# Column tiles of the array for the HGRN scores, and new buffer offsets in SBUF

## The chip, the cores and the metric

One core of a Trainium2 chip. A core has a matrix engine (TensorE, PE in the profile; its weight loads are shown apart as PEld), VectorE (DVE), ScalarE (ACT), GpSimd (POOL) and SyncE (SP), which issues most of the DMAs. They share SBUF, 128 partitions of on-chip memory; TensorE writes to PSUM, 128 partitions of eight banks. The metric is the time of one execution on the device in microseconds, as the median of several runs.

## What is computed

A trunk of two decoder layers on 256 positions of width 2048, float32. Layer 0 mixes positions with an HGRN2 recurrence of 16 heads (key and value width 128), layer 1 with a causal gMLP. After each mixer comes a gated ConvFFN of width 5632; every sub-layer ends in a layer norm of the scaled residual plus the sub-layer. The part that the change touches is the recurrence:

```python
cum = jnp.cumsum(lf_c, axis=2)
rel = cum[:, :, :, None, :] - cum[:, :, None, :, :]
decay = jnp.exp(jnp.where(mask[:, :, None], rel, -jnp.inf))
scores = jnp.einsum('bhtk,bhsk,bhtsk->bhts', q_c, k_c, decay)
out = (jnp.einsum('bhts,bhsv->bhtv', scores, v_c)
       + jnp.einsum('bhtk,bhkv->bhtv', q_c * jnp.exp(cum), state))
```

So the score of query t and key s is a product over the key width in which each channel has decayed from s to t; scores with s after t are zero. The kernel has its own scheme for this: it takes 128 positions at a time and builds the scores in levels.

## The kernel before

**The large matmuls.** Weights come from HBM in chunks of 512 rows by 512 columns (1 MB), one DMA on SyncE's queue each. `convert` (L80) splits a chunk `raw` into a high part `whi` (a cast on ScalarE, L90) and the remainder `wlo` (a subtraction on VectorE, L91); the pool `wp` has three buffers each of `raw`, `hi` and `lo`, and `ahead` (L96) keeps up to three chunks converted ahead of use. The activations stand split in the same way: `X` (input of a sub-layer, transposed) and `Y` (input of its last projection), each as 16 blocks of 128 rows with 256 high and 256 low columns.

`block_a` (L107) has the activations as stationary operand and streams 512 columns of weights: three matmuls in a row, high by high, high by low, low by high (L120 to L122), called a trio here. `block_b` (L147) has the weights as stationary operand and streams the activations: `both` (L156) 512 columns under a high weight, `rest` (L163) 256 columns under a low one; the two are called a pair. A block_b of four chunks has 64 pairs, a block_a of four chunks 32 trios. In the whole program 240 chunks go through block_b (16 pairs each) and 152 through block_a or its staggered form (8 trios each).

**Where the buffers start.** The pool `cp` holds, in the order of the code, a pad of `LINE - 128` bytes, X, Y (32 KB each per partition), z (16 KB), a pad of `PAD1` bytes, then small constants. The pool `wp` follows. A `whi` or `wlo` buffer has `SKEW` elements (of four bytes) more than it needs, so that the three buffers of a tag start 8320 bytes apart.

**The HGRN stage.** `hgrn` (L440) runs four groups of four heads. A group (L457) is a block_b for q, one for f, a block_a for v, two calls of `mix` (L521; two heads and 256 positions each, called halves), a block_b for the gate sg, and the output's norm. The tile framework orders the instructions of all engines ahead of time from dependencies and priorities, so the small matmuls of `mix` stand in TensorE's queue between pairs of the sg block; each engine then takes its queue in order.

**mix.** It works on four 128-position squares th (two heads by two position blocks), with decayed queries Q, keys K and segment decays T. All its matmuls are float32, which the profile records as two instructions each.

- The diagonal, `pd` (L533 to L544): sixteen matmuls of 32 stationary columns by 32 moving ones, each at its own column tile of the array, `tile_position=(0, 32 * j)`, and four predicated copies through the identity into `scores`.
- Three levels, b = 1, 4, 16 (L545 to L587): at each, blocks of 4b positions are joined from four parts. W (L550 to L554) holds the moving columns, 192 for each square; four matmuls (L558) of 128 keys by 192 columns follow, in two PSUM tiles `pl` of two squares each, and six predicated copies (L567) with `mask` put the wanted strips into `scores`. Then Q, K and T are carried to the next level (L571 to L587).
- The last product (L589 to L594): four matmuls of 128 by 128 for the 64 by 64 corner, and a predicated copy with `upper`.
- The product between the two position blocks (`pc`, L604), the product with v (`pout`, L611 to L616), its copy to `o` (L617), and four squares with a running sum on ScalarE into the scratch tile `junk` (L622).

`scores`, set to zero once, has two buffers, one for each half. PSUM's pool `misc` has two banks for all of these; `acc` has six for the large matmuls. `masks` (L415) makes the masks on GpSimd at the start; `bounds` (L278) uses the tile `lbt` in the buffer of tag "sg".

Of the kernel before, what the change touches and what calls it, by code (L numbers as in the profile page):

```python
# [8 lines left out]
F32 = mybir.dt.float32  # L9
F32R = mybir.dt.float32r  # L10
U32 = mybir.dt.uint32
AF = mybir.ActivationFunctionType
ALU = mybir.AluOpType
PSUM = bass.MemoryType.PSUM

P = 128
# [12 lines left out]
LEVELS = (1, 4, 16)  # L29
FFN_GROUPS = (3, 4, 4)  # L30
AHEAD = 3
LINE = 512
PAD1 = 192
SKEW = 32
XSEQ = ((0, 2, 4), (2, 2, 0), (4, 4, 1), (8, 4, 1), (12, 4, 0))
TURN_ACT = 3

# [1 line left out]
class Trunk:  # L39
# [4 lines left out]
    def __init__(self, ctx, tc, a):  # L44
        self.tc = tc
        self.nc = nc = tc.nc
        self.a = a
        self.ctx = ctx
        ent = ctx.enter_context
        self.cp = ent(tc.tile_pool(name="cp", bufs=1))  # L50
        self.wp = ent(tc.tile_pool(name="wp", bufs=3))
        self.acc = ent(tc.tile_pool(name="acc", bufs=6, space=PSUM))
        self.misc = ent(tc.tile_pool(name="misc", bufs=2, space=PSUM))
        cp = self.cp
        cp.tile([P, LINE - 128], mybir.dt.uint8, name="pad0")
        self.X = cp.tile([P, NK, 2, S], F32R, name="X")
        self.Y = cp.tile([P, NK, 2, S], F32R, name="Y")
        self.z = cp.tile([P, 2, D], F32, name="z")
        cp.tile([P, PAD1], mybir.dt.uint8, name="pad1")
        self.small = ent(tc.tile_pool(name="small", bufs=2))  # L60
        self.plan = []
        self.issued = 0
        self.taken = 0
        self.ready = []
# [15 lines left out]
    def convert(self, raw, extra, pieces=2):  # L80
        nc = self.nc
        pool = self.xp if extra else self.wp
        size = CK * NB + (0 if extra else SKEW)
        hi = pool.tile([P, size], F32R, tag="hi", name="whi")
        lo = pool.tile([P, size], F32R, tag="lo", name="wlo")
        hi, lo = (x[:, : CK * NB].rearrange("p (k n) -> p k n", k=CK) for x in (hi, lo))
        n = CK // pieces
        for i in range(0, CK, n):
            s = slice(i, i + n)
            nc.scalar.copy(hi[:, s, :], raw[:, s, :])  # L90
            self.last_lo = nc.vector.tensor_tensor(  # L91
                lo[:, s, :], raw[:, s, :], hi[:, s, :].bitcast(F32), ALU.subtract
            )
        self.ready.append((hi, lo))
# [317 lines left out]
        for c in range(4):  # L412
            self.want(wo, 3 * CK, c * NB, c == 3)

    def masks(self):  # L415


        nc, cp = self.nc, self.cp
        self.mask = {}
        for b in LEVELS:  # L420
            n = P // 4 // b
            m = cp.tile([P, n, 3, b], F32, name=f"mask{b}")
            nc.gpsimd.memset(m, 1.0)
            nc.gpsimd.affine_select(
                out=m, in_=m, pattern=[[-4 * b, n], [-b, 3], [0, b]], compare_op=ALU.is_ge,
                fill=0.0, base=0, channel_multiplier=1,
            )
            nc.gpsimd.affine_select(
                out=m, in_=m, pattern=[[4 * b, n], [b, 3], [0, b]], compare_op=ALU.is_ge,
                fill=0.0, base=b - 1, channel_multiplier=-1,  # L430
            )
            self.mask[b] = m
        self.upper = cp.tile([P, 1], F32, name="upper")
        nc.gpsimd.memset(self.upper, 1.0)
        nc.gpsimd.affine_select(
            out=self.upper, in_=self.upper, pattern=[[0, 1]], compare_op=ALU.is_ge,
            fill=0.0, base=P // 2 - 1, channel_multiplier=-1,
        )

    def hgrn(self):  # L440
        nc, tc = self.nc, self.tc
        w = self.a["hg_w_in"][0]
        with ExitStack() as st:
            hp = st.enter_context(tc.tile_pool(name="hp", bufs=1))
            lp = st.enter_context(tc.tile_pool(name="lp", bufs=2))
            h1 = st.enter_context(tc.tile_pool(name="h1", bufs=1))
            self.load_vectors(h1.tile([P, 8, P], F32, tag="o", name="rows"))
            self.masks()
            scores = []
            for i in range(2):  # L450
                s = h1.tile([P, 3, 2, P], F32, name=f"scores{i}")
                nc.gpsimd.memset(s, 0.0)
                scores.append(s)
            for g in range(4):
                self.hgrn_group(g, w, hp, lp, h1, scores)

# [64 lines left out]
    def mix(self, q, f, k1, v, sc, o, ss, lp, h1):  # L521
# [3 lines left out]

        nc = self.nc
        flat = lambda x: x.rearrange("p h n -> p (h n)")
        own = lambda th: slice((th % 2 * 2 + th // 2) * P, (th % 2 * 2 + th // 2 + 1) * P)
        K, T = flat(k1), flat(f)
        Q = lp.tile([P, 2 * S], F32, tag="Q", name="Q")  # L530
        nc.vector.tensor_tensor(Q, flat(q), T, ALU.mult)
        scv = sc[:, 0:2].rearrange("p t h n -> p (t h) n")
        pd = self.misc.tile([P, 4, 32], F32, tag="m", name="pd")  # L533
        for th in range(4):
            for j in range(4):
                own_j = slice(own(th).start + 32 * j, own(th).start + 32 * j + 32)
                nc.tensor.matmul(
                    pd[32 * j : 32 * j + 32, th, :], K[:, own_j], flat(q)[:, own_j],
                    start=True, stop=True, tile_position=(0, 32 * j),
                )  # L540
        for j in range(4):
            s = slice(32 * j, 32 * j + 32)
            mi = self.ident[s, s].bitcast(U32).unsqueeze(1).to_broadcast([32, 4, 32])
            nc.vector.copy_predicated(scv[s, :, s], mi, pd[s])  # L544
        for b in LEVELS:  # L545
            n = 2 * S // (4 * b)
            seg = lambda x: x.rearrange("p (n i r) -> p n i r", i=4, r=b)
# [2 lines left out]
            W = lp.tile([P, 4, 192], F32, tag="W", name="W", bufs=1)  # L550
# [1 line left out]
            nc.scalar.copy(Wv[:, :, 0:3, :], Qv[:, :, 1:4, :])  # L552
            nc.vector.tensor_tensor(Wv[:, :, 3:5, :], Qv[:, :, 2:4, :], row(Tv[:, :, 1:3]), ALU.mult)
            nc.vector.tensor_tensor(Wv[:, :, 5:6, :], Wv[:, :, 4:5, :], row(Tv[:, :, 1:2]), ALU.mult)  # L554
            for t in range(2):
                pl = self.misc.tile([P, 2, 192], F32, tag="m", name="pl")
                for h in range(2):
                    nc.tensor.matmul(  # L558
                        pl[:, h, :], K[:, own(2 * t + h)], W[:, 2 * h + t, :], start=True, stop=True
                    )  # L560
                at = 0
                for d in (1, 2, 3):
                    w = (4 - d) * b
                    dst = sc[:, t].rearrange("p h (n x) -> p h n x", x=4 * b)[:, :, :, d * b :]
                    src = pl.rearrange("p h (n x) -> p h n x", x=6 * b)[:, :, :, at : at + w]
                    mk = self.mask[b].bitcast(U32)[:, :, 0 : 4 - d, :].rearrange("p n i r -> p n (i r)")
                    nc.vector.copy_predicated(  # L567
                        dst, mk.unsqueeze(1).to_broadcast([P, 2, P // 4 // b, w]), src
                    )
                    at += w  # L570
            G = lp.tile([P, P, 4], F32, tag="G", name="G", bufs=1)[:, :n, :]  # L571
            Tn = lp.tile([P, P], F32, tag="T", name="T")[:, :n]
            mul = lambda out, x, y: nc.vector.tensor_tensor(out, x, y, ALU.mult)
# [12 lines left out]
            mul(seg(Kn)[:, :, 0:2, :], Kv[:, :, 0:2, :], row(G[:, :, 2:4]))  # L586
            Q, K, T = Qn, Kn, Tn  # L587
        b = P // 2
        pl = self.misc.tile([P, 4, P], F32, tag="m", name="pl")  # L589
        for th in range(4):  # L590
            nc.tensor.matmul(pl[:, th, :], K[:, own(th)], Q[:, own(th)], start=True, stop=True)
        nc.vector.copy_predicated(
            scv[:, :, b:], self.upper.bitcast(U32).unsqueeze(2).to_broadcast([P, 4, b]), pl[:, :, b:]
        )  # L594
        seg = lambda x: x.rearrange("p (h t i r) -> p h t i r", h=2, t=2, i=2)
        Tv = T.rearrange("p (h t i) -> p h t i", h=2, t=2)
        Qn = lp.tile([P, 2, 2, b], F32, tag="Q", name="Q")
# [17 lines left out]
            nc.tensor.matmul(po[:, 1, h, :], sc[:, 2, h, :], v[:, 0, c], start=True, stop=False)  # L615
            nc.tensor.matmul(po[:, 1, h, :], sc[:, 1, h, :], v[:, 1, c], start=False, stop=True)  # L616
        nc.scalar.copy(o, po)  # L617
        junk = lp.tile([P, P], F32, tag="junk", name="junk", bufs=1)
        for t in range(2):
            for h in range(2):  # L620
                i = 2 * t + h
# [248 lines left out]
```

## Time and profile before

| | |
|---|---|
| runs, three | 2307.3, 2307.91 and 2308.39 us; median 2307.91 us |
| the profiled execution | 2308.43 us |
| its span, first to last instruction | 2306.7 us |
| granted TensorE clock, mean | 0.998 |
| DMA | 430.07 MB, mean 186 GB/s |
| instructions | 30892 |

The profile comes from one execution, whose span is 1.7 us shorter than its own time; that time is 0.5 us over the median. "Busy" is the time in which an engine had an instruction under way. Matmuls overlap one another, so the recorded duration of one (0.39 us for 512 columns) is longer than the distance from its start to the next start; distances are what a stream costs.

### The profile page before, as it was taken

Reading aid. Unit: us, or ns where it says so; the run is one execution under the profiler, and the core shown is the slowest. Engines: PE = TensorE matmul, PEld = TensorE weight load, DVE = VectorE, ACT = ScalarE, POOL = GpSimd, SP = SyncE. Lnnn points to the kernel's source line nnn. Section 1 sums busy time; section 2 is a strip of 40 time slices with the busy share of each in tenths; the row PEclk is TensorE's granted clock in tenths of the full one; section 3 lists DMA queues with packets and bytes.
Section 4 is the critical chain, followed back from the end, with each engine's and each line's share of the span. In section 5 each row is a group of like instructions: output and inputs, shape, how many; then the busy total and the mean of one; then the engine's idle time right before and its main releaser. Section 6 shows DMA issues by size and latency. Waiting matters only on the chain.

```text
span 2306.7 us, 30892 instructions
## 1 busy us (share of the span) xinstructions
PE 2282.7 (99%) x12333; PEld 1949.8 (85%) x12333; DVE 1505.9 (65%) x2431; ACT 1090.5 (47%) x1642; POOL 43.7 (2%) x86
## 2 busy tenths in 40 slices
PE   8999999999999999999999999999999999999998
PEld 7888888888888888888888888889888888888886
DVE  5868786857775666456665776567765666466655
ACT  5565555536543444334443645445443454344442
POOL 3000000000000000000000000000000000000000
PEclk9999999999999999999999999999999999999999
DMA  7354545464566555555555676655565555555553
GB/s 252 124 195 139 182 136 185 148 233 150 180 214 210 195 184 183 199 179 192 195 185 182 201 223 192 212 177 182 189 231 183 189 187 190 190 193 183 183 201 109
DMA packets 214047, 430.07 MB, mean 186 GB/s; under 512 B 7544, under 2 KB 8336, under 8 KB 213904
## 3 DMA queue, kind: packets, MB, share of 16 engines
q1 hardware_dynamic: 209536, 415.26, 54.1%
q0 software_dynamic: 4368, 12.85, 1.8%
q8 instruction: 96, 1.57, 0.3%
q14 instruction: 47, 0.39, 0.0%
HBM read 425.98 MB, written 2.10 MB: 186 GB/s over the span
## 4 chain that ended last, share of the span: by engine, by line
PE 95%; DVE 4%; ACT 0%; DMA 0%; issue 0%; SPq 0%; DVEq 0%; ACTq 0%
PE pb L156 37%; PE pb L163 19%; PE pa L120 12%; PE pa L121 12%; PE pa L122 12%; DVE scores L567 1%; DVE wlo L91 1%; PE pl L558 1%; PE pt L302 1%; DVE scores L544 0%; PE pg L724 0%; PE pa L647 0%; PE pa L645 0%; PE pa L646 0%; DMA z<-in_x_dram 0%
## 5 line engine op out<-in xcount | busy, mean ns | idle before, releaser
L91 DVE TENSOR_TENSOR wlo<-raw,whi 128x1024 fp32r<-128x1024 f32 (+1 forms) x786 | 930.4, 1219 | 686.6 <-ACT whi L90 678.5
L156 PE MATMUL pb<-X,whi 128*128 128x512 f32 (+1 forms) x3960 | 1335.0, 388 | 1.9 <-DVE X L314 1.9
L90 ACT CAST whi<-raw 128x1024 fp32r<-128x1024 f32 (+1 forms) x786 | 790.0, 1047 | 898.0 <-PE pb L156 418.1
L163 PE MATMUL pb<-X,wlo 128*128 128x256 f32 x3840 | 1053.7, 282 | 0.0
L156 PEld LDWEIGHTS pb<-X,whi 128*128 128x128 f32 x3960 | 725.9, 188 | 156.4 <-DVE X L314 2.3
L163 PEld LDWEIGHTS pb<-X,wlo 128*128 128x128 f32 x3840 | 714.9, 188 | 4.7
L120 PE MATMUL pa<-whi,Y 128*128 128x512 f32 x928 | 367.0, 396 | 0.0
L121 PE MATMUL pa<-wlo,Y 128*128 128x512 f32 x928 | 365.2, 394 | 0.0
L122 PE MATMUL pa<-whi,Y 128*128 128x512 f32 x928 | 364.0, 392 | 0.0
L122 PEld LDWEIGHTS pa<-whi,Y 128*128 128x128 f32 x928 | 174.1, 188 | 42.1
L120 PEld LDWEIGHTS pa<-whi,Y 128*128 128x128 f32 x928 | 174.3, 188 | 40.7
L121 PEld LDWEIGHTS pa<-wlo,Y 128*128 128x128 f32 x928 | 174.4, 188 | 39.0
L201 ACT COPY rest<-pb 128x256 f32<-128x256 f32 x240 | 88.2, 371 | 109.8 <-PE pb L156 94.0
L120 PE MATMUL pa<-whi,X 128*128 128x512 f32 x256 | 101.3, 396 | 0.0
L121 PE MATMUL pa<-wlo,X 128*128 128x512 f32 x256 | 100.9, 394 | 0.0
L122 PE MATMUL pa<-whi,X 128*128 128x512 f32 x256 | 100.4, 392 | 0.0
L775 DVE SCALAR_TENSOR_TENSOR act<-a,cols,act 128x254 f32<-128x254 f32 (+1 forms) x176 | 73.2, 481 | 0.0
L122 PEld LDWEIGHTS pa<-whi,X 128*128 128x128 f32 x256 | 48.0, 188 | 11.5
L120 PEld LDWEIGHTS pa<-whi,X 128*128 128x128 f32 x256 | 48.1, 188 | 11.0
L121 PEld LDWEIGHTS pa<-wlo,X 128*128 128x128 f32 x256 | 48.1, 188 | 10.6
L394 DVE TENSOR_TENSOR z<-z,pa 128x512 f32<-128x512 f32 x40 | 27.4, 684 | 36.1 <-PE pa L122 31.6
L567 DVE COPY_PREDICATED scores<-mask,pl 128x192 f32<-128x192 uint32 (+2 forms) x144 | 40.2, 356 | 2.3 <-PE pl L558 1.8
(161 smaller groups left out, 1083.2 us busy)
## 6 DMA issues: line engine op xcount, KB each, us to landing
raw<-in_ffn_w_up_dram SPq DMA_DIRECT2D x176, 1024.0 KB, 4.9
raw<-in_ffn_w_down_dram SPq DMA_DIRECT2D x88, 1024.0 KB, 4.9
raw<-in_hg_w_in_dram SPq DMA_DIRECT2D x63, 1024.0 KB, 5.4
raw<-in_sg_w_in_dram SPq DMA_DIRECT2D x32, 1024.0 KB, 5.3
raw<-in_hg_w_out_dram SPq DMA_DIRECT2D x16, 1024.0 KB, 4.9
raw<-in_sg_w_out_dram SPq DMA_DIRECT2D x16, 1024.0 KB, 4.9
g<-in_ln_g_dram POOLq DMA_DIRECT2D x16, 256.0 KB, 5.4
b<-in_ln_b_dram POOLq DMA_DIRECT2D x16, 256.0 KB, 7.7
```

The source lines that it names most:

```text
L90: nc.scalar.copy(hi[:, s, :], raw[:, s, :])
L91: self.last_lo = nc.vector.tensor_tensor(lo[:, s, :], raw[:, s, :], hi[:, s, :].bitcast(F32), ALU.subtract)
L120: nc.tensor.matmul(ps[t], xh, hi[:, kk, :], start=n[t] == 0, stop=False)
L121: nc.tensor.matmul(ps[t], xh, lo[:, kk, :], start=False, stop=False)
L122: nc.tensor.matmul(ps[t], xl, hi[:, kk, :], start=False, stop=last)
L156: nc.tensor.matmul(ps[j][:, :, s], ch[0][:, k % CK, c], act[:, k, :, s], start=start and k == 0, stop=k == last, skip_group_check=halves,)
L163: nc.tensor.matmul(ps[j][:, 1, :], ch[1][:, k % CK, c], act[:, k, 0, :], start=False, stop=False, skip_group_check=halves,)
L201: nc.scalar.copy(r, ps[:, 1, :])
L302: nc.tensor.transpose(ps[:, j, :], self.z[:, t, k * P : (k + 1) * P], self.ident)
L394: nc.vector.tensor_tensor(zz, zz, ps, ALU.add)
L567: nc.vector.copy_predicated(dst, mk.unsqueeze(1).to_broadcast([P, 2, P // 4 // b, w]), src)
L775: nc.vector.scalar_tensor_tensor(cv[:, d:], x[:, : S - d], self.c(("cw", l, 2 - d), f), cv[:, d:], ALU.mult, ALU.add,)
```

## The change

**Scores in compact blocks.** Each level's product is now taken in column tiles of the array. At b = 1 and b = 4 a tile has 32 keys and the 48 columns of W that belong to those 32 positions; at b = 16 it has 64 keys and 96 columns. `blocks` issues them, four (or two) column tiles for each square; pd uses the same helper. All four squares of a level share one `pl` tile. The results go by three predicated copies a level into `near32` (four 32-column blocks) and `near64` (four 64-column blocks), with masks cut to that form; pd takes one copy, with `diag`. `widen` copies near32 into the diagonal of near64 before the copies of level 16 (four ScalarE copies), and near64 into `scores` before the last product (two). The last product is four matmuls of 64 by 64 at tile (0, 0), put into `scores` by a ScalarE copy without a mask.

**Small tiles.** The full masks are temporary, in the buffer of tag "sg", and are copied on GpSimd into the compact ones: 14 copies. `upper` is gone. `junk` shares the one buffer of W.

**Buffer offsets.** LINE goes from 512 to 256, SKEW from 32 to 16 elements, PAD1 from 192 to 160; a pad of 192 bytes stands between X and Y, and one of 64 bytes between the high and the low weight buffers. By the sizes, the buffers of a tag are then 8256 bytes apart, and the high and low buffer of a chunk start at equal addresses modulo 256.

```diff
-LINE = 512
-PAD1 = 192
-SKEW = 32
+LINE = 256
+PAD_Y = 192
+PAD1 = 160
+SKEW = 16
+BLOCK = {1: 32, 4: 32, 16: 64}
...
         self.X = cp.tile([P, NK, 2, S], F32R, name="X")
+        cp.tile([P, PAD_Y], mybir.dt.uint8, name="pady")
         self.Y = cp.tile([P, NK, 2, S], F32R, name="Y")
...
         hi = pool.tile([P, size], F32R, tag="hi", name="whi")
+        if not extra:
+            pool.tile([P, LINE - 3 * 4 * SKEW], mybir.dt.uint8, tag="gap", name="gap", bufs=1)
         lo = pool.tile([P, size], F32R, tag="lo", name="wlo")
...
-            m = cp.tile([P, n, 3, b], F32, name=f"mask{b}")
+            m = h1.tile([P, n, 3, b], F32, tag="sg", name=f"mask{b}")
...
-            self.mask[b] = m
+            w = BLOCK[b]
+            self.mask[b] = cp.tile([P, n * w // P, 3, b], F32, name=f"block{b}")
+            for i in range(P // w):
+                s = slice(i * w, (i + 1) * w)
+                nc.gpsimd.tensor_copy(
+                    self.mask[b][s], m[s, i * n * w // P : (i + 1) * n * w // P]
+                )
+        self.diag = cp.tile([P, 32], F32, name="diag")
+        for i in range(4):
+            s = slice(32 * i, 32 * i + 32)
+            nc.gpsimd.tensor_copy(self.diag[s], self.ident[s, s])
...
+        def blocks(ps, n, K, moving):
+
+            for th in range(4):
+                for j in range(P // n):
+                    nc.tensor.matmul(
+                        ps[n * j : n * j + n, th, :], K[:, own(th, n, j)], moving(th, j),
+                        start=True, stop=True, tile_position=(0, n * j),
+                    )
+
+        def widen(out, src, n, m):
+
+            for j in range(P // n):
+                at = j * n % m
+                nc.scalar.copy(out[n * j : n * j + n, :, at : at + n], src[n * j : n * j + n])
...
+        blocks(pd, 32, K, lambda th, j: flat(q)[:, own(th, 32, j)])
+        nc.vector.copy_predicated(
+            near[32], self.diag.bitcast(U32).unsqueeze(1).to_broadcast([P, 4, 32]), pd
+        )
...
+            w = BLOCK[b]
+            pl = self.misc.tile([P, 4, 3 * w // 2], F32, tag="m", name="pl")
+            blocks(pl, w, K, lambda th, j: W[:, swap(th), 3 * w // 2 * j : 3 * w // 2 * (j + 1)])
+            if w == 64:
+                widen(near64, near32, 32, 64)
+            at = 0
+            for d in (1, 2, 3):
+                m = (4 - d) * b
+                dst = near[w].rearrange("p a (n x) -> p a n x", x=4 * b)[:, :, :, d * b :]
+                src = pl.rearrange("p a (n x) -> p a n x", x=6 * b)[:, :, :, at : at + m]
+                mk = self.mask[b].bitcast(U32)[:, :, 0 : 4 - d, :].rearrange("p n i r -> p n (i r)")
+                nc.vector.copy_predicated(
+                    dst, mk.unsqueeze(1).to_broadcast([P, 4, w // 4 // b, m]), src
+                )
+                at += m
...
-        pl = self.misc.tile([P, 4, P], F32, tag="m", name="pl")
+        widen(scv, near64, 64, P)
+        pl = self.misc.tile([b, 4, b], F32, tag="m", name="pl")
         for th in range(4):
-            nc.tensor.matmul(pl[:, th, :], K[:, own(th)], Q[:, own(th)], start=True, stop=True)
-        nc.vector.copy_predicated(
-            scv[:, :, b:], self.upper.bitcast(U32).unsqueeze(2).to_broadcast([P, 4, b]), pl[:, :, b:]
-        )
+            nc.tensor.matmul(
+                pl[:, th, :], K[:, own(th, b)], Q[:, own(th, b, 1)], start=True, stop=True,
+                tile_position=(0, 0),
+            )
+        nc.scalar.copy(scv[:b, :, b:], pl)
...
-        junk = lp.tile([P, P], F32, tag="junk", name="junk", bufs=1)
+        junk = lp.tile([P, P], F32, tag="W", name="junk", bufs=1)
```

More of the change, by code (lines that the diff above doesn't have):

```diff
@@ L413, in plan_hgrn, with masks @@
             self.want(wo, 3 * CK, c * NB, c == 3)
-    def masks(self):
+    def masks(self, h1):
         nc, cp = self.nc, self.cp
@@ L431, in masks @@
             )
-            self.mask[b] = m
[L433 to L437, printed above, removed]
-        )
+            w = BLOCK[b]
[9 more added lines that the diff above has]
+            nc.gpsimd.tensor_copy(self.diag[s], self.ident[s, s])
     def hgrn(self):
@@ L447, in hgrn @@
             self.load_vectors(h1.tile([P, 8, P], F32, tag="o", name="rows"))
-            self.masks()
+            self.masks(h1)
             scores = []
             for i in range(2):
-                s = h1.tile([P, 3, 2, P], F32, name=f"scores{i}")
-                nc.gpsimd.memset(s, 0.0)
-                scores.append(s)
+                sc = [
+                    h1.tile([P, *n], F32, name=f"{name}{i}")
+                    for name, n in (("scores", (3, 2, P)), ("near32", (4, 32)), ("near64", (4, 64)))
+                ]
+                for s in sc:
+                    nc.gpsimd.memset(s, 0.0)
+                scores.append(sc)
             for g in range(4):
@@ L527, in mix, with own @@
         flat = lambda x: x.rearrange("p h n -> p (h n)")
-        own = lambda th: slice((th % 2 * 2 + th // 2) * P, (th % 2 * 2 + th // 2 + 1) * P)
+        swap = lambda th: th % 2 * 2 + th // 2
+        def own(th, n=P, j=0):
+            at = swap(th) * P + j * n
+            return slice(at, at + n)
+        def blocks(ps, n, K, moving):
[9 more added lines that the diff above has]
+                nc.scalar.copy(out[n * j : n * j + n, :, at : at + n], src[n * j : n * j + n])
+        sc, near32, near64 = sc
+        near = {32: near32, 64: near64}
         K, T = flat(k1), flat(f)
@@ L533, in mix @@
         pd = self.misc.tile([P, 4, 32], F32, tag="m", name="pd")
[L534 to L544, printed above, removed]
+        blocks(pd, 32, K, lambda th, j: flat(q)[:, own(th, 32, j)])
+        nc.vector.copy_predicated(
+            near[32], self.diag.bitcast(U32).unsqueeze(1).to_broadcast([P, 4, 32]), pd
+        )
         for b in LEVELS:
@@ L554, in mix @@
             nc.vector.tensor_tensor(Wv[:, :, 5:6, :], Wv[:, :, 4:5, :], row(Tv[:, :, 1:2]), ALU.mult)
[L555 to L570, printed above, removed]
+            w = BLOCK[b]
[13 more added lines that the diff above has]
+                at += m
             G = lp.tile([P, P, 4], F32, tag="G", name="G", bufs=1)[:, :n, :]
@@ L588, in mix @@
         b = P // 2
-        pl = self.misc.tile([P, 4, P], F32, tag="m", name="pl")
+        widen(scv, near64, 64, P)
+        pl = self.misc.tile([b, 4, b], F32, tag="m", name="pl")
         for th in range(4):
-            nc.tensor.matmul(pl[:, th, :], K[:, own(th)], Q[:, own(th)], start=True, stop=True)
-        nc.vector.copy_predicated(
-            scv[:, :, b:], self.upper.bitcast(U32).unsqueeze(2).to_broadcast([P, 4, b]), pl[:, :, b:]
-        )
+            nc.tensor.matmul(
[3 more added lines that the diff above has]
+        nc.scalar.copy(scv[:b, :, b:], pl)
         seg = lambda x: x.rearrange("p (h t i r) -> p h t i r", h=2, t=2, i=2)
```

## The prediction

> **What bounds the kernel now.** I read the page first: engine shares, then the chain that ended last.
>
> ```profile
> span 2306.7 us, 30892 instructions
> PE 2282.7 (99%) x12333; PEld 1949.8 (85%) x12333; DVE 1505.9 (65%) x2431; ACT 1090.5 (47%) x1642; POOL 43.7 (2%) x86
> PE 95%; DVE 4%; ACT 0%; DMA 0%; issue 0%; SPq 0%; DVEq 0%; ACTq 0%
> ```
>
> TensorE is the bound: it is hardly ever without a matmul, and 95% of the chain runs on it. So an edit pays by what it takes out of TensorE's own stream; time taken from VectorE or ScalarE pays only where TensorE waits for them. The edits to the mixer act in the recurrent stage alone, so I asked the windows view for one of its four groups (stretch: its length, PE busy, PEld, DVE, ACT, POOL, clock, DMA share, GB/s).
>
> ```profile
> 252.40:358.70 106.30, 105.65 (x650) 91.45 (x649) 81.34 (x196) 58.34 (x112) 0.00 (x0) 1.00 0.49 159
> ```
>
> TensorE is full there too (105.65 of 106.30 us), at full clock, while VectorE is at 77% and ScalarE at 55%. The chain in order of time marks the start of a block_b wherever one block_b follows another:
>
> ```profile
> 760.40 0.46 PE pb L156 x2
> ...
> 894.49 0.46 PE pb L156 x2
> ...
> 1028.21 0.46 PE pb L156 x2
> ```
>
> Six blocks lie between the first two rows: 134.09 / 6 = 22.35 us each, or 0.3492 us for each of 64 pairs "both, rest". Between the last two lie one block_b before the projection, one after it, and four block_a of four chunks: (133.72 - 44.70) / 128 = 0.6955 us for each trio of block_a.
>
> A group is three block_b and one block_a, so 4 x 22.3 = 89.3 of its 106.3 us. The other 17 us are the small float32 matmuls of two calls of mix, their entry and exit, and short waits. That is all that the column tiles can reach: 4 x 17 = 68 us.
>
> **The matmuls of mix.** Timeline of TensorE, group 0 (start, duration, line; a long name xN is N instructions in a row):
>
> ```profile
> 83.82 0.40 PE L122 MATMUL pa<-whi,X 128*128 128x512 f32 x1
> 84.15 0.46 PE L537 MATMUL pd<-q,k 128*32 128x32 f32 x32
> 84.53 0.92 PE L558 MATMUL pl<-W,k 128*128 128x192 f32 x4
> ...
> 94.02 1.52 PE L558 MATMUL pl<-W,K 128*128 128x192 f32 x8
> 95.24 0.53 PE L156 MATMUL pb<-X,whi 128*128 128x512 f32 x1
> 95.61 0.28 PE L163 MATMUL pb<-X,wlo 128*128 128x256 f32 x1
> ...
> 96.34 1.13 PE L591 MATMUL pl<-Q,K 128*128 128x128 f32 x8
> 97.30 0.50 PE L606 MATMUL pc<-Q,K 128*128 128x128 f32 x3
> ...
> 100.23 0.46 PE L537 MATMUL pd<-q,k 128*32 128x32 f32 x32
> 100.62 0.38 PE L163 MATMUL pb<-X,wlo 128*128 128x256 f32 x1
> 100.84 0.40 PE L156 MATMUL pb<-X,whi 128*128 128x512 f32 x1
> 102.60 0.89 PE L558 MATMUL pl<-W,k 128*128 128x192 f32 x4 [0.36 <-DVE scores L544]
> ```
>
> What goes: one level is four matmuls of 128x192, recorded as 8 instructions. From 94.02 to 95.61 is 1.59 us, less the 0.23 us that a 512-column matmul takes in the stream (a third of a trio): 1.36 us, 0.17 us an instruction. Three levels make 4.08 us. The 8 of L591 take 97.30 - 96.34 = 0.96 us. Together **5.04 us per mix**.
>
> What comes has a precedent in the trace: pd is already sixteen 32-column tiles. Its 32 instructions take 84.53 - 84.15 = 0.38 us. Entry costs 84.15 - 83.82 - 0.23 = 0.10 us, exit 100.84 - 100.62 - 0.12 = 0.10 us (0.12 is a rest's share of a pair). So a visit costs 0.58 us. An instruction streams 0.17 / 192 = 0.0009 us a column; four 32-column tiles side by side need 0.028 us, and eight such groups 0.23 us. The fixed part is 0.58 - 0.23 = 0.35 us. If the four tiles ran one after the other, 32 instructions would need 0.91 us, so the row shows that they run together.
>
> New levels: b=1 and b=4, 32 instructions of 48 columns in eight groups: 8 x 0.0425 + 0.35 = 0.69 us each. b=16, 16 instructions of 96 columns in eight pairs: 8 x 0.085 + 0.35 = 1.03 us. The last product, 8 instructions of 64 columns, all at tile (0, 0) and so in a row: 8 x 0.057 + 0.20 for entry and exit = 0.66 us. Sum 3.07 us. **Saved: 5.04 - 3.07 = 2.0 us a mix, 16 us for eight mixes.** Ends: without any fixed part it would be 3.3 us a mix, 26 us; with no tile beside another each level would cost 32 x 0.0425 + 0.35 = 1.7 us and the sum be 5.8 us, 0.8 us a mix or 6 us in all more than now.
>
> The Trainium skill, "TensorE: Matmul & The Clock Gate", section "Wait - 56ns, not 53.3ns?", speaks against so many small matmuls: start to start never drops below about 25 ns, however few the columns. By it 32 instructions would need an estimated 0.80 us, each 48-column level about 0.4 us more than above, the gain about 10 us and the time an estimated 2295 us. The trace disagrees: 32 instructions in 0.38 us is 12 ns each, in tiles side by side.
>
> Waits: the last row above waits 0.36 us for a pl bank that copy_predicated has yet to empty. A level needed two banks of the two there are; now it needs one. Such waits stand in the first level of the second half of each group; with the lesser ones I put them at 0.8 us a group and take **3 us** for four groups (0 to 6).
>
> **VectorE and ScalarE.** Groups by line and shape:
>
> ```profile
> L567 DVE COPY_PREDICATED scores<-mask,pl 128x192 f32<-128x192 uint32 x48 | 18.7, 402 | 2.1 <-PE pl L558 1.8
> ...
> L567 DVE COPY_PREDICATED scores<-mask,pl 128x64 f32<-128x64 uint32 x48 | 13.4, 310 | 0.0
> L544 DVE COPY_PREDICATED scores<-ident,pd 32x128 f32<-32x128 uint32 x32 | 9.5, 296 | 10.6 <-PE pd L537 10.2
> ```
>
> ```profile
> L584 ACT COPY K<-K 128x128 f32<-128x128 f32 x16 | 4.7, 294 | 7.8 <-DVE K L573 7.8
> L610 ACT COPY scores<-pc 128x256 f32<-128x256 f32 x8 | 3.0, 374 | 9.2 <-PE pc L606 9.2
> ```
>
> VectorE: 0.72 ns an element and 0.264 us fixed, from the two L567 rows. Eighteen copies a mix (6.4 us) become nine: two levels of 96, 64 and 32 elements (0.93 us each) and one of 192, 128 and 64 (1.07 us), 2.9 us in all. Four L544 (1.18 us) become one of 0.36 us. That is 4.3 us a mix less, and the last copy leaves as well. ScalarE gains four copies of 128 elements and three of 256: 4 x 0.294 + 3 x 0.374 = 2.3 us a mix, 4.6 us a group on 58 us. I count both at nothing: TensorE's filler, the 22 us block_b of sg, hides them. Were that cover gone, 4.3 us less on VectorE would be a gain, 2.3 us more on ScalarE a loss.
>
> New waits: the widening copies wait on ScalarE for VectorE's copy_predicated, and behind them stand casts of whi; weights are taken up to three chunks ahead, 5.6 us each. And junk now lies in W's only buffer, so the second half's first W must wait until the first half's squares are done:
>
> ```profile
> 99.12 0.61 ACT L552 COPY W<-Q 128x384 f32<-128x384 f32 x1 [0.74 <-DVE Q L531]
> ...
> 102.84 0.19 ACT L622 ACTIVATION_READ_ACCUMULATOR junk<-o 128x1 f32 x1
> ```
>
> That moves W from 99.12 to 103.03, 3.9 us a group. VectorE's L553 follows it, and behind L553 its wlo subtractions. TensorE has block_b to fill with, so I count nothing and keep 4 x 3.9 = 16 us as the other end.
>
> At the start GpSimd makes 14 small copies more, and lbt now shares the temporary masks' buffer:
>
> ```profile
> 21.94 0.74 POOL L452 MEMSET scores<- 128x768 f32 x1
> ```
>
> ```profile
> 40.26 0.17 DVE L283 TENSOR_TENSOR lbt<-cols 128x16 f32<-128x16 f32 x1
> ```
>
> At 0.74 us each, 14 copies end some 10 us after 22.7, at 33 us; lbt is wanted at 40.26. Nothing.
>
> **The addresses.** By the tile sizes, X and Y start today at multiples of 512, the three high buffers at 0, 128, 256 and the low ones at 384, 0, 128 modulo 512. Modulo 256 the slots are (0, 128), (128, 0), (0, 128). After: X at 0, Y at 192, and high and low both at 0, 64, 128. Timeline of TensorE, first matmuls of successive chunks:
>
> ```profile
> 610.04 0.39 PE L156 MATMUL pb<-X,whi 128*128 128x512 f32 x1
> ...
> 615.59 0.39 PE L156 MATMUL pb<-X,whi 128*128 128x512 f32 x1
> 615.94 0.40 PE L156 MATMUL pb<-X,whi 128*128 128x512 f32 x1
> 616.30 0.40 PE L156 MATMUL pb<-X,whi 128*128 128x512 f32 x1
> ...
> 621.22 0.39 PE L156 MATMUL pb<-X,whi 128*128 128x512 f32 x1
> ```
>
> ```profile
> 682.50 0.39 PE L120 MATMUL pa<-whi,Y 128*128 128x512 f32 x1
> ...
> 687.99 0.40 PE L120 MATMUL pa<-whi,Y 128*128 128x512 f32 x1
> ...
> 693.58 0.40 PE L120 MATMUL pa<-whi,Y 128*128 128x512 f32 x1
> ```
>
> The same 16 pairs take 5.55 us from one slot and 5.63 us from the next (0.347 and 0.352 a pair); the same eight trios 5.49 and 5.59 us (0.686 and 0.699). The slot with high at 128 costs more in block_b and less in block_a. So addresses count, by one or two per cent, and not by a rule that I can read off; no row has equal offsets in these slots. With 240 chunks of block_b (3840 pairs) and 152 of block_a (1216 trios): all at the lower cost -9 and -12 us, all at the higher cost +10 and +4 us. I take **0**, between -21 and +14.
>
> The Trainium skill, "SBUF - State Buffer", section "Who interferes with whom", has TensorE wait on nobody for SBUF and names no rule on addresses; by it this part is worth exactly nothing, which leaves the sum as it is. The trace disagrees in the small: 5.49 against 5.59 us for the same work.
>
> **Sum.** The profiled execution took 2308.4 us. 2308.4 - 16 - 3 + 0 = 2289.4 us; it lay 0.5 us above the median, so **2289 us**.
>
> **Rivals.**
> - Addresses help: all slots at the lower cost. For it: those costs occur, in turn. Against: no slot has both. 2289 - 21 = 2268; half of it, 2278.
> - A new wait takes the gain: W behind the squares, TensorE out of filler. 2289 + 16 = 2305. Against: 22 us of block_b stand beside each pair of mixes.
> - The change doesn't do what it says: at 48 and 96 columns the tiles run one after the other. 2308.4 + 6 - 3 - 0.5 = 2311. Against: the pd rows, with tiles of the same width of weights.
> - Slower: the new offsets put the alternation of block_b, in all slots, at its long step. 615.94 to 616.30 is such a step, 0.36 us. 3840 x (0.360 - 0.349) = +42 us, 2331 us. It decides from a mean pair of 0.349 + 19/3840 = 0.354 us on. Against: that slot's mean is 0.352, as short steps follow long ones.
>
> **How the numbers follow.** Forecast, addresses within 10 us of nothing: 0.58. Addresses help by more than that: 0.18. New wait: 0.10; no overlap: 0.04. Long steps: 0.10. The range 2268 to 2306 takes in all but the last two cases and a little below. About 0.2% (4.6 us) is what a measurement of this kernel can tell from no change. Faster: the first two and some of the third, 0.79; same 0.12; slower 0.09.
>
> **What would show it.** Right: 32 tile instructions of 48 columns within 0.5 us; groups of about 102 us; VectorE's copies near 2.9 us a mix; block_b still near 22.35 us and trios near 0.696. Wrong: tile instructions 25 ns or more apart; TensorE waiting for W or pl in mix; blocks whose length differs from 22.35 us by more than 0.15 us, which is the addresses.

## The result, and the profile after

| | before | changed |
|---|---|---|
| median | 2308.16 us (2307.3 to 2309.08, 6 runs) | 2296.85 us (2296.24 to 2297.07, 6 runs) |
| the profiled execution, its span | 2308.43, 2306.7 us | 2296.34, 2294.6 us |

The ratio is 0.995, with a 95% interval from 0.9937 to 0.9963: the change saves 11.3 us, where 19 were forecast. The time lies in the stated range.

The page of the changed kernel, in the rows that were shown of before (line numbers are those of the new code: L161 and L168 are the pair, L125 to L127 the trio, L552 is `blocks`):

```profile
span 2294.6 us, 31751 instructions
PE 2272.9 (99%) x12781; PEld 1930.8 (84%) x12781; DVE 1473.2 (64%) x2327; ACT 1104.6 (48%) x1698; POOL 48.5 (2%) x102
PE 97%; DVE 1%; ACT 1%; DMA 1%; SPq 0%; issue 0%; DVEq 0%; ACTq 0%
```

The bound is the same engine, more purely than before: VectorE's share of the chain went from 4% to 1%. The windows view of one HGRN group:

```profile
218.90:320.80 101.90, 101.72 (x762) 86.06 (x760) 73.43 (x170) 62.33 (x126) 0.00 (x0) 1.00 0.51 166
```

A group lasts 101.9 us instead of 106.3: 4.4 us less, some 18 us in four groups. So the recurrent stage alone would have given nearly all that was forecast, and something took 6 us back elsewhere. The chain in order of time shows where:

```profile
741.85 0.47 PE pb L161 x2
...
877.13 0.47 PE pb L161 x2
...
1011.07 0.47 PE pb L161 x2
```

Read as in the prediction: six blocks in 135.28 us are 22.55 us each, 0.3523 us a pair (before 0.3492). The stretch to the third row, less two such blocks, leaves (133.94 - 45.09) / 128 = 0.6941 us a trio (before 0.6955). On average over these blocks a block_b has become 0.2 us longer, more than the 0.15 us that the prediction had named as the sign that the addresses count.

TensorE's timeline in group 0:

```profile
85.10 0.39 PE L161 MATMUL pb<-X,whi 128*128 128x512 f32 x1
85.42 0.55 PE L552 MATMUL pl<-W,K 128*32 128x48 f32 x32
85.90 0.50 PE L168 MATMUL pb<-X,wlo 128*128 128x256 f32 x2
...
88.30 0.88 PE L552 MATMUL pl<-W,K 128*64 128x96 f32 x16
89.01 0.63 PE L620 MATMUL pl<-Q,K 128*64 128x64 f32 x8
89.57 0.39 PE L168 MATMUL pb<-X,wlo 128*128 128x256 f32 x1
...
93.72 0.46 PE L552 MATMUL pd<-q,k 128*32 128x32 f32 x32
...
99.31 0.55 PE L552 MATMUL pl<-W,k 128*32 128x48 f32 x32
```

A level of 32 instructions takes 0.48 us (85.42 to 85.90), that of 16 takes 0.71, the last product 0.56. And in the second half 5.6 us pass between pd (93.72) and the first level (99.31). In the kernel before, the first level followed pd (at 100.23 there) within 0.9 us:

```profile
101.08 0.82 PE L558 MATMUL pl<-W,k 128*128 128x192 f32 x4
```

What stands between is W behind the squares, as ScalarE's timeline of the changed kernel shows:

```profile
97.58 0.19 ACT L652 ACTIVATION_READ_ACCUMULATOR junk<-o 128x1 f32 x1
97.80 0.60 ACT L581 COPY W<-Q 128x384 f32<-128x384 f32 x1
```

Groups of the copies:

```profile
L595 DVE COPY_PREDICATED near<-block,pl 128x64 f32<-128x64 uint32 x24 | 5.9, 247 | 0.0
...
L595 DVE COPY_PREDICATED near<-block,pl 128x96 f32<-128x96 uint32 x16 | 4.5, 282 | 1.4 <-PE pl L552 0.9
L595 DVE COPY_PREDICATED near<-block,pl 128x32 f32<-128x32 uint32 x16 | 3.9, 243 | 0.0
...
L595 DVE COPY_PREDICATED near<-block,pl 128x192 f32<-128x192 uint32 x8 | 2.9, 365 | 0.0
L571 DVE COPY_PREDICATED near<-diag,pd 128x128 f32<-128x128 uint32 x8 | 2.4, 299 | 10.1 <-PE pd L552 10.1
...
L595 DVE COPY_PREDICATED near<-block,pl 128x128 f32<-128x128 uint32 x8 | 2.3, 292 | 0.0
```

```profile
L561 ACT COPY near<-near 32x128 f32<-32x128 f32 x32 | 9.5, 295 | 0.6
L561 ACT COPY scores<-near 64x256 f32<-64x256 f32 x16 | 6.5, 404 | 0.1
...
L624 ACT COPY scores<-pl 64x256 f32<-64x256 f32 x8 | 2.9, 366 | 1.9 <-PE pl L620 1.5
```

### The profile page after: what moved, and what is told of

Read it like the earlier page. It is cut to its first block, busy times and chain, and to the rows that moved or that the text cites. A ratio compares the mean times of both kernels' runs of the same rounds, so it can differ in the third digit from the quotient of the medians.

```text
span 2294.6 us, 31751 instructions
## 1 busy us (share of the span) xinstructions
PE 2272.9 (99%) x12781; PEld 1930.8 (84%) x12781; DVE 1473.2 (64%) x2327; ACT 1104.6 (48%) x1698; POOL 48.5 (2%) x102
## 4 chain that ended last, share of the span: by engine, by line
PE 97%; DVE 1%; ACT 1%; DMA 1%; SPq 0%; issue 0%; DVEq 0%; ACTq 0%
PE pb L161 38%; PE pb L168 20%; PE pa L125 12%; PE pa L127 12%; PE pa L126 12%; PE pl L552 1%; DMA z<-in_x_dram 1%; DVE wlo L96 0%; PE pt L307 0%; PE pg L754 0%; PE pa L677 0%; PE pa L675 0%; PE pa L676 0%; PE po L524 0%; PE pout L644 0%; ACT whi L95 0%
## 5 line engine op out<-in xcount | busy, mean ns | idle before, releaser
L161 PE MATMUL pb<-X,whi 128*128 128x512 f32 (+1 forms) x3960 | 1344.3, 390 | 1.9 <-DVE X L319 1.9
L168 PE MATMUL pb<-X,wlo 128*128 128x256 f32 x3840 | 1055.8, 283 | 0.0
L161 PEld LDWEIGHTS pb<-X,whi 128*128 128x128 f32 x3960 | 725.6, 188 | 164.5 <-DVE X L319 2.4
L168 PEld LDWEIGHTS pb<-X,wlo 128*128 128x128 f32 x3840 | 714.8, 188 | 6.5
L125 PE MATMUL pa<-whi,Y 128*128 128x512 f32 x928 | 366.2, 395 | 0.0
L127 PE MATMUL pa<-whi,Y 128*128 128x512 f32 x928 | 365.8, 394 | 0.0
L127 PEld LDWEIGHTS pa<-whi,Y 128*128 128x128 f32 x928 | 174.6, 188 | 40.6
L125 PEld LDWEIGHTS pa<-whi,Y 128*128 128x128 f32 x928 | 174.6, 188 | 39.0
L125 PE MATMUL pa<-whi,X 128*128 128x512 f32 x256 | 101.0, 394 | 0.0
L127 PE MATMUL pa<-whi,X 128*128 128x512 f32 x256 | 100.6, 393 | 0.0
L127 PEld LDWEIGHTS pa<-whi,X 128*128 128x128 f32 x256 | 48.1, 188 | 11.0
L125 PEld LDWEIGHTS pa<-whi,X 128*128 128x128 f32 x256 | 48.1, 188 | 10.3
L809 ACT ACTIVATE act<-act 128x256 f32<-128x256 f32 x88 | 33.8, 415 | 7.8 <-DVE act L805 7.6
```

The costliest lines, as they stand in the source:

```text
L125: nc.tensor.matmul(ps[t], xh, hi[:, kk, :], start=n[t] == 0, stop=False)
L127: nc.tensor.matmul(ps[t], xl, hi[:, kk, :], start=False, stop=last)
L161: nc.tensor.matmul(ps[j][:, :, s], ch[0][:, k % CK, c], act[:, k, :, s], start=start and k == 0, stop=k == last, skip_group_check=halves,)
L168: nc.tensor.matmul(ps[j][:, 1, :], ch[1][:, k % CK, c], act[:, k, 0, :], start=False, stop=False, skip_group_check=halves,)
L809: nc.scalar.activation(cv, cv, AF.Silu)
```

## The experiments

Two theories stood at the start. **A**: the column tiles gained about what was forecast, and the new offsets cost 8 to 10 us in the large matmuls of the whole program. **B**: the offsets are worth nothing, and the tiles gained only 11 us, as ScalarE's new copies and W's new wait hold TensorE up.

### Each half of the change by itself

`tiles_only` is the changed kernel with the offsets of before (all of them moved by the same amount, to fit):

```diff
-LINE = 256
-PAD_Y = 192
-PAD1 = 160
-SKEW = 16
+LINE = 256
+PAD1 = 352
+SKEW = 32
...
-        cp.tile([P, LINE - 128], mybir.dt.uint8, name="pad0")
...
-        cp.tile([P, PAD_Y], mybir.dt.uint8, name="pady")
...
-        if not extra:
-            pool.tile([P, LINE - 3 * 4 * SKEW], mybir.dt.uint8, tag="gap", name="gap", bufs=1)
```

> The column tiles with the offsets of the kernel before (X and Y at equal offsets; high and low slots at (0,128), (128,0), (0,128) modulo 256 from X). Theory A: the tiles won about 20 us and the new offsets gave 8 back, as a pair of block_b went from 0.349 to 0.352 us. Then pairs are back at 0.349, a block_b at 22.35 us, trios at 0.695, and the time is 2288 to 2289 us. Theory B: the tiles won only 11 us, since ScalarE's copies and W behind the squares held TensorE up, and the offsets are worth nothing: 2296 to 2297 us.

Measured 2288.5 us (ratio 0.9916, interval 0.9902 to 0.9929). The chain in order of time of this kernel:

```profile
739.82 0.46 PE pb L156 x2
...
873.91 0.46 PE pb L156 x2
...
1007.63 0.46 PE pb L156 x2
```

Again 134.09 / 6 = 22.35 us a block and 0.6955 us a trio: the very numbers of before.

`offsets_only` is the kernel before with the new offsets:

```diff
-LINE = 512
-PAD1 = 192
-SKEW = 32
+LINE = 256
+PAD_Y = 192
+PAD1 = 0
+SKEW = 16
...
+        cp.tile([P, PAD_Y], mybir.dt.uint8, name="pady")
...
+        if not extra:
+            pool.tile([P, LINE - 3 * 4 * SKEW], mybir.dt.uint8, tag="gap", name="gap", bufs=1)
```

> The kernel before with the new offsets and none of the column tiles. Theory A: pairs at 0.352 us, a block_b 22.55 us, trios at 0.694; 2308 + 11 - 2 = 2315 to 2318 us, slower than before. Theory B (offsets worth nothing): 2308 us, pairs at 0.349.

Measured 2317.11 us (ratio 1.0038, interval 1.0026 to 1.0051). The same view:

```profile
762.04 0.47 PE pb L160 x2
...
897.32 0.47 PE pb L160 x2
...
1031.26 0.47 PE pb L160 x2
```

135.28 / 6 and 133.94 us are the numbers of the changed kernel to the last digit. The two halves add up: -19.5 us for the tiles and +9.2 us for the offsets make -10.3, against -11.3 for the whole; the 1.0 us between them is about as much as the runs of one kernel spread. Theory A holds, and B falls.

### What the offsets do

In the table, "slot (h, l)" is the offset of the high and of the low buffer from X, modulo 256, and Y's is given beside it. Pairs and trios are worked out from three chain rows of each run, as above. The pairs read X. The trios between those rows read Y, so what they see is the slot less Y's offset: (64,64), (128,128) and (192,192) in the change, (128,0) in all_0_128, (128,192) in all_0_64.

`all_0_128` makes the three slots alike:

```diff
-PAD_Y = 192
-PAD1 = 160
-SKEW = 16
+PAD_Y = 128
+PAD1 = 224
+SKEW = 0
...
-            pool.tile([P, LINE - 3 * 4 * SKEW], mybir.dt.uint8, tag="gap", name="gap", bufs=1)
+            pool.tile([P, 128], mybir.dt.uint8, tag="gap", name="gap", bufs=1)
```

> The column tiles, with all three slots alike: high at 0 and low at 128 modulo 256 from X, and Y 128 after X modulo 256. If a slot's cost is set by its offsets from what stands on the other side of the array (high 0, low 128 was the cheaper class of pairs, and high 128, low 0 from the stationary side the cheaper class of trios), pairs come to 0.348 to 0.349 us and trios to 0.688 to 0.690: 2280 to 2285 us. If the order of unequal slots is what counts, or the absolute offset, it lies anywhere from 2285 to 2300 us.

`low_sweep` gives the skew to the low buffers alone (gap 64, no pad before Y, PAD1 96):

> A table: all high slots at 0 from X and Y, low ones at 64, 128 and 192 modulo 256. Theory A: the three slots differ in their pairs by 0.002 us or more, and the slot at (0,128) is at 0.349 as before. If equal offsets of high and low are what costs, all three are below 0.352. If only offsets from X count and not those between high and low, no forecast for 64 and 192. The time lies between 2283 and 2300 us.

`low_64_sweep` keeps the skew and sets the gap to 128 (PAD_Y 128, PAD1 224), so that each low buffer is 64 above its high one modulo 256:

> The column tiles, low always 64 above high modulo 256; slots (0,64), (64,128), (128,192) from X, and Y at 128. Theory A (the distance from high to low sets a pair): all three slots at 0.346 to 0.349 us. Rival (each offset from X counts by itself): slots spread by 0.003 us or more. Trios: Y sees (128,192), (192,0), (0,64); no forecast but 0.686 to 0.700 us. Time 2275 to 2290 us.

`all_0_64` has no skew and a gap of 64 (PAD_Y 128, PAD1 224), `all_0_0` neither skew nor gap nor pad before Y (PAD1 96):

> The column tiles, all slots high 0 and low 64 from X, Y at 128 modulo 256. If a slot keeps its cost when all are alike, pairs 0.347 us, 8 us less than with (0,128): 2274 us with trios as there (0.689), 2282 us with trios at 0.697. If pairs settle higher when no slot differs, as (0,128) did (0.3494 alike, 0.348 mixed), 2280 to 2288 us.

> The column tiles with no skew, no gap and no pad before Y: all slots and X and Y at equal offsets modulo 256. Theory A, by the slots of the changed kernel: pairs at (0,0) 0.353 us, trios at (0,0) 0.686: against the tiles with the old offsets (0.3492 and 0.6955) 3840 x 0.0038 - 1216 x 0.0095 = +15 - 12, 2291 us. Rival (what costs is that the slots differ, not their offsets): pairs at 0.347 to 0.349, 2276 to 2283 us.

| run | slots | Y | pair, us | trio, us | time, us |
|---|---|---|---|---|---|
| tiles_only | (0,128) (128,0) (0,128) | 0 | 0.3492 | 0.6955 | 2288.5 |
| the change | (0,0) (64,64) (128,128) | 192 | 0.3523 | 0.6941 | 2296.85 |
| all_0_128 | (0,128) three times | 128 | 0.3497 | 0.6867 | 2282.31 |
| all_0_64 | (0,64) three times | 128 | 0.3471 | 0.6933 | 2279.27 |
| all_0_0 | (0,0) three times | 0 | 0.3532 | 0.6800 | 2282.63 |
| low_sweep | (0,64) (0,128) (0,192) | 0 | by slot, below | | 2286.35 |
| low_64_sweep | (0,64) (64,128) (128,192) | 128 | by slot, below | | 2286.42 |

The rows of all_0_64 and of all_0_0, the two ends for pairs:

```profile
738.35 0.47 PE pb L161 x2
...
871.65 0.47 PE pb L161 x2
...
1004.82 0.47 PE pb L161 x2
```

```profile
737.33 0.46 PE pb L157 x2
...
872.97 0.46 PE pb L157 x2
...
1005.22 0.46 PE pb L157 x2
```

133.30 / 6 = 22.22 us a block in the first, 135.64 / 6 = 22.61 us in the second; but the four block_a between the last two rows take 133.17 - 44.43 = 88.7 us in the first and 132.25 - 45.21 = 87.0 us in the second. The layout that is worst for pairs is the best for trios. Sorted by slot, with the few steps left out that other work lengthens, the starts of the two sweeps' matmuls give pairs of 0.3473, 0.3493 and 0.3502 us in low_sweep, and 0.3473, 0.3506 and 0.3472 us in low_64_sweep. In the same way the three slots of the change give 0.3528, 0.3529 and 0.3510 us, and those of tiles_only 0.3477, 0.3519 and 0.3481 us.

What follows: the forecasts by slot were good to 0.001 us for pairs in four of the five runs. The distance from high to low matters, but doesn't decide alone. The two dearest slots, (0,0) and (64,64) at 0.353 us, have distance 0; yet (128,128) costs 0.351 and (128,0), at a distance of 128, 0.352. At the same distance of 64 the slot (64,128) is 0.003 us longer than its neighbours, so theory A's simple form in low_64_sweep was wrong and its rival, that each offset counts, nearer. all_0_64 came out between its two times: pairs as forecast, trios (0.6933 us) between the two values that it had allowed. For trios the tables didn't carry over: all_0_0 came out 8 us under its forecast. Its time lies in the range of its rival, but by other means, as the pairs of 0.3532 us are what the rival had excluded.

A slot named modulo 256 isn't one class, either. (0,128) gives 0.348 us a pair in tiles_only, but 0.3494 in all_0_128 and 0.3493 in low_sweep. By the sizes, its low buffer starts 24960 bytes (3 x 8320) above the high one in tiles_only and 24704 (3 x 8192 + 128) in the other two, a difference of 256. Whether the three slots are alike, as in all_0_128, or not, as in low_sweep, made no difference. In the same way a block_a that reads X, whose trios at (0,0) take 0.687 us in the changed kernel and 0.681 in all_0_0, has 24832 bytes (3 x 8256 + 64) from high to low in the first and 24576 in the second. So a table of slots needs the distance from high to low modulo 512 at least. No run varied that alone, and the forecast of all_0_0 took a value from the one distance to the other. Why offsets cost what they do, which bank or port meets which, and whether other engines' accesses to the same buffers play a part, none of these runs shows; that stays open.

### Did the mixer lose anything?

`junk_apart` is the changed kernel with the scratch tile of the squares in the buffers of `sig`:

```diff
-        junk = lp.tile([P, P], F32, tag="W", name="junk", bufs=1)
+        junk = lp.tile([P, S], F32, tag="sig", name="junk")[:, :P]
```

> The changed kernel with the squares' scratch tile in the buffers of sig instead of W's, so that the second half's W needn't wait for the squares. If TensorE's filler hides that wait: 2296 to 2298 us, no change. If the wait held TensorE up: up to 16 us less.

Measured 2295.04 us (2294.56 to 2295.28; ratio to before 0.9945, interval 0.993 to 0.9959), 1.8 us under the changed kernel, whose runs don't overlap with these. Timeline of TensorE:

```profile
94.25 0.46 PE L552 MATMUL pd<-q,k 128*32 128x32 f32 x32
95.86 0.55 PE L552 MATMUL pl<-W,k 128*32 128x48 f32 x32
```

The first level follows pd by 1.6 us instead of 5.6. Of the 4 us a group that W waited, then, 3.5 were hidden by the sg block and 0.45 were not.

`widen_twice` makes each widening copy twice:

```diff
-                nc.scalar.copy(out[n * j : n * j + n, :, at : at + n], src[n * j : n * j + n])
+                for _ in range(2):
+                    nc.scalar.copy(out[n * j : n * j + n, :, at : at + n], src[n * j : n * j + n])
```

> The changed kernel with each of the six widening copies of a mix made twice on ScalarE, some 1.9 us a mix more. If they are hidden: 2296 to 2298 us. If ScalarE's copies hold TensorE up: as much again as they cost now, up to 8 x 1.9 = 15 us more.

Measured 2303.11 us, 6.3 us more than the changed kernel, for 16 us more work on ScalarE (8 x (4 x 0.295 + 2 x 0.404)). Waits of TensorE in this run (total us, times, longest):

```profile
PE pc L637 <- ACT K L633: 3.0, 8, 0.4
...
PE pout L645 <- ACT scores L562: 0.8, 3, 0.3
```

Neither wait is in the same list of the changed kernel; together they make 3.8 of the 6.3 us. So ScalarE's queue has little room left: a first set of copies is covered, a second isn't. Is the first wholly covered? `best_offsets` is all_0_64 with the scratch tile apart; `widen_vector` and `widen_gpsimd` are the same with `nc.vector.tensor_copy` and `nc.gpsimd.tensor_copy` in `widen`.

> The column tiles, all slots (0,64) with Y at 128, and the squares' scratch tile apart from W. If the two gains add: 2279.3 - 1.8 = 2277 to 2278 us. If the 1.8 us belonged to the offsets of the changed kernel: 2279 us.

> The same as best_offsets with the six widening copies of a mix on VectorE instead of ScalarE. Doubling them on ScalarE cost 6.3 us. If that is ScalarE's queue standing before the last products of mix (K for pc, scores for pout), and the single copies cost in proportion, 2272 to 2275 us. If only the doubled copies were too much for the cover, or VectorE's queue is as long: 2277 to 2280 us.

> The same with the six widening copies on GpSimd, which does nothing else in this stage. If the queues of ScalarE and VectorE are what counts: 2272 to 2275 us. If GpSimd's copies are so long that pout waits for scores: 2278 to 2290 us.

best_offsets took 2277.32 us (ratio to before 0.9868, interval 0.9854 to 0.9881): the two gains add. widen_vector took 2278.22 us and widen_gpsimd 2294.96 us. Moving the copies off ScalarE gained nothing, so as they are they cost nothing that can be had back in this way. On GpSimd they are too long; its group and TensorE's wait:

```profile
L561 POOL COPY scores<-near 64x256 f32<-64x256 f32 x16 | 13.6, 853 | 12.9 <-DVE near L595 10.4 <-DVE W L582 2.0
```

```profile
PE pout L644 <- POOL scores L561: 10.5, 8, 2.0
```

853 ns a copy instead of ScalarE's 404, and pout waits 10.5 us for them. That is not all of the 17.6 us over best_offsets, and the time is above what either forecast gave. The rest fits the clock: the windows view has a granted clock of 0.50 from 105.62 to 109.03 us, and in one such stretch of 3.41 us in each of the other three groups, where best_offsets has 1.00. At half the clock four such stretches lose some 4 x 1.7 = 6.8 us, an estimate from these rows; 10.5 + 6.8 = 17.3 us. Each stretch begins within 0.5 us of the end of a wait of 1.97 us for pout, the longest of a group; behind the wait of 0.91 us in group 0 the clock stays at 1.00. The traces show that the two come together, not what takes the clock down.

## Why the prediction was right, and by how much it was off

- **The tiles, -16 us, and the waits, -3 us.** Right in mechanism and sum: -19.5 us in tiles_only. By parts, without entry and exit: a 48-column level was put at 0.49 us and took 0.48; the level of 16 at 0.83 and took 0.71; the last product at 0.46 and took 0.56. The fixed share worked out from pd's rows carried over to 48 columns; the errors of the other two cancel, which is luck. TensorE's idle time before the matmuls of pl fell from 2.6 us in all to 0.6 in tiles_only, 2 of the 3 us of waits. As tiles_only also bears the 1.8 us of W's wait (below), tiles and waits together were worth some 21 us, 2 more than forecast; that tiles_only met the forecast of 2289 us to 0.5 us is luck in this part.
- **The addresses, 0 between -21 and +14.** This is the term that was mis-sized: the prediction chose 0 from the middle of what two classes of slots had shown, and it is +9 us (offsets_only), by the distances pairs +11.9 us (3840 x 0.0031) and trios -1.7 us. Equal offsets of high and low were a class that the trace of before did not have, so neither sign nor size could be read there, and a missing row was taken for an average one. With this term at +9 us and W's wait at +1.8, the forecast of 2289 would have been 2300 us, 3 above the measured time. The rival that addresses help had the wrong sign for these offsets, but all_0_64, 9.2 us under tiles_only, shows that other offsets do help.
- **ScalarE's copies, 0.** Right as to the price: the copies came to 2.35 us a mix (4 x 0.295 + 2 x 0.404 + 0.366 for the last product), 2.3 in the forecast, and they are hidden as far as widen_vector can tell. The cover is thinner than "22 us of block_b" made it look, as widen_twice shows.
- **VectorE's copies.** Nine of them came to 2.45 us a mix, where 2.9 were worked out. The straight line through the old shapes failed at equal size already: a copy of 128x192 took 365 ns where the row of before has 402, one of 128x64 247 where it has 310. Which difference between the two forms makes a copy cheaper wasn't tested. Off TensorE's path it gave nothing that shows apart.
- **W behind the squares, 0, at most 16 us.** It cost 1.8 us: the wait came, 4 us a group, and the filler hid most of it.
- **The 25 ns of the Trainium skill** ("TensorE: Matmul & The Clock Gate", section "Wait - 56ns, not 53.3ns?") don't bind column tiles here: 0.48 us for 32 instructions (16 matmuls) is 15 ns each. In the trace the 32 start in groups of four, 6 to 7 ns apart within a group, and all groups but the first follow at 42.5 ns, the 0.0425 us that the prediction had for four tiles side by side.
- **The slower rival** had the right direction, longer pairs in all three slots, at under a third of its size: 0.3523 us, with the break-even at 0.354. No slot stood at its long step of 0.360 us; the dearest mean was 0.3529.

## What to carry to other kernels

A change with two halves that act on different stages should be priced by stage, and measured by halves: here a gain of 19.5 us hid a loss of 9 us, and the version with only the better half, or with offsets chosen anew (2277 us), beats both kernels. Where a matmul stream makes up nearly all of the time, a distance that is off by 3 ns a pair can undo much of a stage's clean-up (here 12 of 19.5 us), so read the stream's distance from block starts before and after. A class of layout that no row shows isn't average; give it the whole range, and try it by itself.

## What was not expected of the hardware

The distance of one large matmul to the next depends on where its operands start in SBUF. Moving a high and its low buffer together by 256 bytes against X changed little (two slots of tiles_only, 0.3477 and 0.3481 us a pair); moving the low one by 256 bytes against the high one went with 0.348 against 0.3494 us. In all there were pairs from 0.347 to 0.353 us, trios from 0.680 to 0.6955 us, in runs that differ in nothing but pads. No layout tried is best for both kinds of block: with all buffers at equal offsets trios are shortest and pairs longest. The Trainium skill, "SBUF — State Buffer", section "Who interferes with whom", has TensorE wait on no other engine; the runs don't contradict that, as TensorE's own two operands could be what meets, but they show that its time isn't independent of SBUF's layout. And four column tiles side by side keep their overlap with 48 columns: 32 instructions in 0.48 us, in float32.
